# The product of probabilities and values in two attentions: high and low parts of the transposed probabilities side by side in one matmul, the halves summed by a VectorE reduction

## The chip, the core and the metric

The kernel runs on one NeuronCore of a Trainium2 chip. The metric is the device time of one execution in microseconds (us), taken as the median over several executions; lower is better. The kernel before takes 2276.8 us (three runs, 2276.53 to 2277.06). The core has engines that run in parallel and wait for each other through semaphores: TensorE (PE in the profile; PEld is its weight load), VectorE (DVE), ScalarE (ACT), GpSimd (POOL), and SyncE (SP), which issues most of the DMAs. Each engine works through its own instructions in the order in which the program lists them.

## What is computed

Two layers of an encoder on 1024 tokens of width 1024, in float32. Layer 0 mixes tokens with multi-head latent attention (mixer A), layer 1 with differential attention (mixer B); both have 8 heads, values of width 128, and a mask by chunks of 64 tokens. After each mixer and each SwiGLU there is a residual and a LayerNorm. Cut to the attentions:

```
# mixer A
logits = einsum(q_nope, k_nope) + einsum(q_rope, k_rope)
p = softmax(where(chunk_mask, logits * scale, -1e30))
o = einsum('bhqk,bkhd->bqhd', p, v)          # then o @ w_o
...
# mixer B
p = softmax(where(chunk_mask, logits * scale - slope * dist, -1e30))   # two maps per head
a = p[:, 0] - lam * p[:, 1]
o = einsum('bhqk,bkhe->bqhe', a, v)          # then rmsnorm(o) @ w_o
...
h = layernorm(ALPHA * h + mix)
h = layernorm(ALPHA * h + swiglu(h))
```

The change concerns the two products of the probabilities with the values v.

## The kernel before

**High and low parts.** TensorE's operands here have the type fp32r (so named in the profile's rows). Each operand x is split into a high part (x copied to fp32r by ScalarE) and a low part (x minus the high part, by VectorE or GpSimd), and a product becomes three matmuls that add into one PSUM tile: high by high, high by low, low by high.

**Stages.** The program runs through the latent projections, attention A (from 94 us to about 350 us of the profile), its output projection and layer 0's SwiGLU, attention B (from 1145 to about 1552 us), its output projection and layer 1's SwiGLU.

**One attention.** `attention` (L268) walks over heads h and blocks i of 128 queries, 64 steps in all. For each step there are three pieces:

- `score` (L1281 for A, L1428 for B) calls `softmax_block` (L216). PE multiplies queries by keys into PSUM tiles tagged "s"; DVE adds the bias and takes the running maximum (L229), which frees the "s" tile; ACT takes the exponential (L232); DVE the reciprocal of the sum (L234); in A, POOL scales the row (L1290), in B, POOL and DVE combine the two maps (L1440, L1441).
- `turn` calls `transpose_block` (L237). PE transposes the 128x128 probability blocks into a PSUM tile (L160), ACT copies them out as the high part (L253), DVE subtracts to give the low part (L254). Before, the two parts are two SBUF tiles, `pth` and `ptl`, each [128, 2 key blocks, 256 queries].
- `mix` (L1296 and L1447) runs once for every two query blocks, that is for each group g of 256 queries. It calls `pv_group` (L256), which goes over the nj = 2g+2 key blocks that the mask lets through; each has three matmuls with 256 columns into one PSUM tile [128, 256]: vh by hi, vh by lo, vl by hi. The last key block concerns only the second half of the queries, so its three matmuls have 128 columns. Over 8 heads and g = 0 to 3 there are 160 key blocks in each attention, 32 of them last ones.

The PSUM tile is then read out. In A, ACT copies it (L1300) to an SBUF tile `ob` (two buffers), which a DMA on SP's queue stores to `o_dr`. In B, DVE copies it (L1450) to the resident `bo`, from which ACT squares it for the norm (L1465). The product's PSUM tiles come from `ps_o` (L123): in A from the three buffers tagged "m", which the projections use too, in B from a single buffer tagged "o". All of these PSUM tiles are 512 columns wide, of which the product used 256.

**What sets the order.** The program is written with a tile framework. It places each instruction on its engine by a simulated timeline and by priorities (`high_priority` at L280 and L282), so that the pieces of several steps, and the projections of the next head that `fill` hands in, are woven together; when durations or dependencies of some pieces differ, the places of others move too. On each engine the resulting order is fixed, and an instruction that waits holds up all that stand behind it on that engine.

Of the kernel before, what the change touches and what calls it, by code (L numbers as in the profile page):

```python
# [10 lines left out]
F32R = mybir.dt.float32r  # L11
AF = mybir.ActivationFunctionType
ALU = mybir.AluOpType
# [3 lines left out]
P = 128  # L17
# [25 lines left out]
def trunk(  # L43
# [33 lines left out]
    V, A, G, T = nc.vector, nc.scalar, nc.gpsimd, nc.tensor  # L77
# [45 lines left out]
    def ps_o(name):  # L123
        return ps.tile([P, 512], F32, tag="o", bufs=ps_bufs[3], name=name) if len(ps_bufs) > 3 else ps_m(name)
# [112 lines left out]
    def transpose_block(ptp, pts, l, i, name):  # L237
        qc = (i % 2) * P
        for jq in range(i // 4 + 1):
            nj = min(4, i + 1 - 4 * jq)  # L240
            pt = ps_t(f"pt_{name}_{jq}")
            for jj in range(nj):
                j = 4 * jq + jj
                tr(pt[:, jj * P:(jj + 1) * P], l[:, j * P:(j + 1) * P])
            for jp in range(2 * jq, 2 * jq + (nj + 1) // 2):
                n = min(2, i + 1 - 2 * jp)
                if i % 2 == 0:
                    pts[jp] = tuple(
                        ptp.tile([P, 2, 256], F32R, tag=f"pt{c}", name=f"pt{c}_{name}_{jp}") for c in "hl"
                    )  # L250
                src = pt[:, (jp % 2) * 256:(jp % 2) * 256 + n * P].rearrange("p (j q) -> p j q", j=n)
                hv, lv = (t[:, :n, qc:qc + P] for t in pts[jp])
                newest["hi"] = A.copy(hv, src).ins  # L253
                newest["lo"] = V.tensor_tensor(lv, src, f32(hv), ALU.subtract).ins  # L254

    def pv_group(pts, g, v_of, name):  # L256
        po = ps_o(f"o_{name}")
        nj = 2 * g + 2
        for j in range(nj):
            hi, lo = pts[j // 2]  # L260
            vh, vl = v_of(j)
            c = slice(P, 256) if j == nj - 1 else slice(0, 256)
            first, last = j == 0, j == nj - 1
            for a, b, st, sp_ in ((vh, hi, first, False), (vh, lo, False, False), (vl, hi, False, last)):
                T.matmul(po[:, c], a, b[:, j % 2, c], start=st, stop=sp_, skip_group_check=True)
        return po

    def attention(score, turn, mix, fill, la, hp):  # L268
# [918 lines left out]
    lv = [late[:, 64 * i:64 * i + 64] for i in range(4)]  # L1187
# [16 lines left out]
    with ast as st:  # L1204
# [3 lines left out]
        ptp = st.enter_context(tc.tile_pool(name="a1p", bufs=5, side="right", reuse_waits="tile"))  # L1208
        vt, qr, qn, kn, wts, lt, pts = {}, {}, {}, {}, {}, {}, {}
# [86 lines left out]
        def mix_a(h, g):  # L1296
            hc = slice((h % 2) * P, (h % 2) * P + P)
            po = pv_group(pts.pop((h, g)), g, lambda j: tuple(v[:, hc] for v in vt[h // 2, j]), f"a{h}_{g}")
            ob = vp.tile([P, 256], F32, tag="ob", name=f"ob{h}_{g}", bufs=2)
            A.copy(ob, po[:, :256])  # L1300
            nc.sync.dma_start(o_dr[0][g][h], ob)

        fill = {}
# [12 lines left out]
        for h in range(1, H):  # L1316
            b = 8 * (h - 1)
# [45 lines left out]
    with ExitStack() as st:  # L1363
        lp = st.enter_context(tc.tile_pool(name="b1l", bufs=5, reuse_waits="tile"))
        pool = st.enter_context(tc.tile_pool(name="b1", bufs=2, reuse_waits="tile"))
        ptp = st.enter_context(tc.tile_pool(name="b1p", bufs=4, reuse_waits="tile"))
        bb = pool.tile([P, S], F32, tag="bb", name="bb", bufs=1)
        nc.sync.dma_start(bb, c_bias_b)
        vt, lt, pts, sqs, q_slot = {}, {}, {}, {}, {}
        qt = [big_tile(f"bq{j}") for j in range(2)]  # L1370
        kt = [big_tile(f"bk{j}") for j in range(2)]
        ob = big_tile("bo", F32)
# [74 lines left out]
        def mix_b(h, g):  # L1447
            hc = slice((h % 2) * P, (h % 2) * P + P)
            po = pv_group(pts.pop((h, g)), g, lambda j: tuple(v[:, hc] for v in vt[h // 2, j]), f"b{h}_{g}")
            V.tensor_copy(o_rows(h, g), po[:, :256])  # L1450

        def o_rows(h, g, n=1):

            return ob[:, h % 2, g * 256:(g + n) * 256]
# [182 lines left out]
```

## Time and profile before

| | |
|---|---|
| median of 3 runs | 2276.8 us |
| the profiled execution | 2275.05 us |
| its span, first to last instruction | 2273.3 us |
| PE busy, share of the span | 2245.0 us, 99% |
| DVE busy | 1550.6 us, 68% |
| ACT busy | 1016.7 us, 45% |
| POOL busy | 862.6 us, 38% |
| mean granted TensorE clock | 0.998 of full speed |

The profile is one execution. Its times count from the start of the span. In a row of the timeline the first number is the start of an instruction and the second its duration; matmuls overlap in these rows, each starting before the one ahead of it has ended, so that what a matmul costs a busy PE is the distance from its start to the next start, and not the duration in its row. A group row ends with busy time in us, the mean duration in ns, and the idle time of the engine just before its instructions with what ended it.

### The profile page before, as it was taken

The numbers are of one execution on the slowest core, as the hardware profiler recorded it, in microseconds if no ns is written. First come the engines' busy times: TensorE is split into PE (matmuls) and PEld (weight loads), VectorE is DVE, ScalarE is ACT, GpSimd is POOL, SyncE is SP. The second block draws the span as 40 slices with busy tenths as digits, with TensorE's granted clock in tenths as the row PEclk, the third lists the DMA queues.
The fourth block names the chain that finished last, engine by engine and source line by source line (L and its number), as shares of the span: only waits on it lengthen the run. The fifth ranks groups of instructions, "written<-read, shape, count | busy, mean of one in ns | idle before, by whom it ended". The sixth has DMA issues, their size and how long they took to land. (4 is left out here: it accounts for less than half of the span.)

```text
span 2273.3 us, 31157 instructions
## 1 busy us (share of the span) xinstructions
PE 2245.0 (99%) x11426; PEld 1914.2 (84%) x11426; DVE 1550.6 (68%) x2909; ACT 1016.7 (45%) x2101; POOL 862.6 (38%) x673
## 2 busy tenths in 40 slices
PE   9999999999999999999999999999999999999998
PEld 9898998888888888888888898987778888888886
DVE  6666665596656668778476667576587666668778
ACT  4465664352333334445465656555442333334443
POOL 2233452114444446555232424221014444446562
PEclk9999999999999999999999999999999999999999
DMA  5121325334313238554310212153344223247554
GB/s 206 41 97 59 119 98 186 139 140 140 126 70 139 70 126 323 196 179 167 107 47 23 67 38 70 26 208 116 125 153 152 94 98 111 96 156 271 181 179 149
DMA packets 104281, 289.33 MB, mean 127 GB/s; under 512 B 8640, under 2 KB 31808, under 8 KB 93632
## 3 DMA queue, kind: packets, MB, share of 16 engines
q1 hardware_dynamic: 100128, 277.90, 34.8%
q0 software_dynamic: 4000, 9.44, 1.5%
q8 instruction: 90, 1.47, 0.3%
q14 instruction: 63, 0.52, 0.1%
HBM read 205.78 MB, written 77.33 MB: 125 GB/s over the span
## 5 line engine op out<-in xcount | busy, mean ns | idle before, releaser
L511 ACT CAST op_g<-gr 128x512 fp32r<-128x512 f32 x240 | 147.5, 622 | 404.7 <-PE gb L555 225.2
L511 POOL TENSOR_TENSOR op_g<-gr,op_g 128x512 fp32r<-128x512 f32 x104 | 146.0, 1408 | 300.6 <-DVE tmp L649 160.5
L511 DVE TENSOR_TENSOR op_h<-rh,op_h 128x512 fp32r<-128x512 f32 x154 | 163.7, 1092 | 61.2 <-ACT op_h L511 61.1
L555 PE MATMUL ga<-xh_m,op_g 128*128 128x512 f32 x512 | 168.1, 389 | 0.0
L511 ACT CAST op_h<-rh 128x512 fp32r<-128x512 f32 x154 | 92.5, 619 | 145.8 <-DMA rh<-h_dr 39.4
L858 PE MATMUL dw<-op_w_t,op_h 128*128 128x512 f32 x660 | 151.9, 390 | 0.0
L858 PEld LDWEIGHTS dw<-op_w_t,op_h 128*128 128x128 f32 x660 | 123.3, 188 | 25.6
L232 ACT ACTIVATE l_b<-l_b,mx_b 128x256 f32<-128x256 f32 (+7 forms) x128 | 99.5, 778 | 75.9 <-DVE mx_b L229 74.0
L511 POOL TENSOR_TENSOR op_w_t<-tt,op_w_t 128x512 fp32r<-128x512 f32 x66 | 99.9, 1516 | 82.6 <-ACT op_w_t L511 78.1
L1440 POOL TENSOR_SCALAR l_b<-l_b,r_b,cst 128x128 f32<-128x128 f32 (+3 forms) x64 | 52.5, 821 | 204.8 <-DVE r_b L234 198.8
L858 PE MATMUL dx<-op_w_b,op_h 128*128 128x512 f32 x528 | 120.3, 389 | 0.0
L858 PEld LDWEIGHTS dx<-op_w_b,op_h 128*128 128x128 f32 x528 | 99.1, 188 | 20.6
L555 PE MATMUL gc<-t1h_f,op_g 128*128 128x512 f32 x352 | 116.2, 391 | 0.0
L555 PE MATMUL gb<-t4h_f,op_g 128*128 128x512 f32 x352 | 115.7, 390 | 0.5 <-DVE tmp L640 0.5
L511 DVE TENSOR_TENSOR op_g<-gr,op_g 128x512 fp32r<-128x512 f32 x136 | 110.2, 810 | 8.7 <-ACT op_g L511 8.2
L555 PE MATMUL gc<-b22h_f,op_g 128*128 128x512 f32 x352 | 115.5, 389 | 0.0
L555 PE MATMUL gb<-t3h_f,op_g 128*128 128x512 f32 x352 | 115.2, 389 | 0.0
L555 PE MATMUL gb<-t2h_f,op_g 128*128 128x512 f32 x352 | 115.1, 389 | 0.0
L511 POOL TENSOR_TENSOR op_g<-s,op_g 128x512 fp32r<-128x512 f32 x40 | 54.7, 1368 | 156.1 <-ACT op_g L511 156.0
L555 PEld LDWEIGHTS ga<-xh_m,op_g 128*128 128x128 f32 x512 | 96.1, 188 | 19.9
L155 PE MATMUL bp<-xT_f,h_wb 128*128 128x512 f32 x256 | 102.8, 402 | 0.0
L157 PE MATMUL bp<-xT_f,l_wb 128*128 128x512 f32 x256 | 101.6, 397 | 0.0
(389 smaller groups left out, 6738.4 us busy)
## 6 DMA issues: line engine op xcount, KB each, us to landing
gr<-in_w_gu SPq DMA_DIRECT2D x44, 1024.0 KB, 6.8
rh<-h_dr SPq DMA_DIRECT2D x28, 1024.0 KB, 5.2
h_dr<-sh SPq DMA_DIRECT2D x22, 1024.0 KB, 4.9
h_dr<-hp SPq DMA_DIRECT2D x22, 768.0 KB, 4.0
tt<-in_w_dn SPq DMA_DIRECT2D x22, 512.0 KB, 8.3
rh<-h_dr SPq DMA_DIRECT2D x14, 768.0 KB, 4.3
z<-xs_dr SPq DMA_DIRECT2D x16, 512.0 KB, 11.2
rw_b<-in_w_dn SPq DMA_DIRECT2D x8, 1024.0 KB, 8.8
```

Of the source, the lines that this page charges most:

```text
L155: T.matmul(ps_out, lh, rh, start=(i == 0), stop=False)
L157: T.matmul(ps_out, ll, rh, start=False, stop=(i == n - 1))
L232: newest["exp"] = A.activation(l[:, :n], l[:, :n], AF.Exp, bias=mx, scale=-1.0, accum_out=sm).ins
L511: return A.copy(hi, src).ins, eng.tensor_tensor(lo, src, f32(hi), ALU.subtract).ins
L555: T.matmul(o, w[:, a, kc], x[b][:, k, :], start=(first and k == 0 and (a, b) == (0, 0)), stop=(k == 3 and a == 1), skip_group_check=True,)
L858: i = T.matmul(o, h[:, a, c], w[:, b_], start=(first and (a, b_) == (0, 0)), stop=(last and a == 1), skip_group_check=True,).ins
L1440: G.tensor_scalar(l1[:, :n], l1[:, :n], r1, nlam, ALU.mult, ALU.mult)
```

## The change

The high and low parts become one SBUF tile `pt` of shape [128, 2 parts, 2 key blocks, 256 queries]. For each key block, one matmul with vh as weights takes both parts as its moving operand (two runs of 256 columns) and writes 512 columns of PSUM: the first 256 hold vh by hi, the second 256 vh by lo. A second matmul with vl as weights adds vl by hi to the first 256 columns. For the last key block the two matmuls have 2x128 and 128 columns. So there are 640 matmuls where there were 960, with as many columns as before. The halves are summed when the tile is read out, by one VectorE `tensor_reduce` over 512 columns whose innermost step is from one half to the other; it replaces ACT's copy in A and DVE's copy in B.

```
--- before.py
+++ after.py
@@ -245,24 +245,21 @@
             for jp in range(2 * jq, 2 * jq + (nj + 1) // 2):
                 n = min(2, i + 1 - 2 * jp)
                 if i % 2 == 0:
-                    pts[jp] = tuple(
-                        ptp.tile([P, 2, 256], F32R, tag=f"pt{c}", name=f"pt{c}_{name}_{jp}") for c in "hl"
-                    )
+                    pts[jp] = ptp.tile([P, 2, 2, 256], F32R, tag="pt", name=f"pt_{name}_{jp}")
                 src = pt[:, (jp % 2) * 256:(jp % 2) * 256 + n * P].rearrange("p (j q) -> p j q", j=n)
-                hv, lv = (t[:, :n, qc:qc + P] for t in pts[jp])
+                hv, lv = (pts[jp][:, a, :n, qc:qc + P] for a in range(2))
                 newest["hi"] = A.copy(hv, src).ins
                 newest["lo"] = V.tensor_tensor(lv, src, f32(hv), ALU.subtract).ins
 
     def pv_group(pts, g, v_of, name):
-        po = ps_o(f"o_{name}")
+        po = ps_o(f"o_{name}").rearrange("p (a q) -> p a q", a=2)
         nj = 2 * g + 2
         for j in range(nj):
-            hi, lo = pts[j // 2]
+            pt = pts[j // 2][:, :, j % 2]
             vh, vl = v_of(j)
             c = slice(P, 256) if j == nj - 1 else slice(0, 256)
-            first, last = j == 0, j == nj - 1
-            for a, b, st, sp_ in ((vh, hi, first, False), (vh, lo, False, False), (vl, hi, False, last)):
-                T.matmul(po[:, c], a, b[:, j % 2, c], start=st, stop=sp_, skip_group_check=True)
+            T.matmul(po[:, :, c], vh, pt[:, :, c], start=(j == 0), stop=False, skip_group_check=True)
+            T.matmul(po[:, 0, c], vl, pt[:, 0, c], start=False, stop=(j == nj - 1), skip_group_check=True)
         return po
 
     def attention(score, turn, mix, fill, la, hp):
@@ -1297,7 +1294,7 @@
             hc = slice((h % 2) * P, (h % 2) * P + P)
             po = pv_group(pts.pop((h, g)), g, lambda j: tuple(v[:, hc] for v in vt[h // 2, j]), f"a{h}_{g}")
             ob = vp.tile([P, 256], F32, tag="ob", name=f"ob{h}_{g}", bufs=2)
-            A.copy(ob, po[:, :256])
+            V.tensor_reduce(ob, po.rearrange("p a q -> p q a"), mybir.AxisListType.X, ALU.add)
             nc.sync.dma_start(o_dr[0][g][h], ob)
 
         fill = {}
@@ -1447,7 +1444,7 @@
         def mix_b(h, g):
             hc = slice((h % 2) * P, (h % 2) * P + P)
             po = pv_group(pts.pop((h, g)), g, lambda j: tuple(v[:, hc] for v in vt[h // 2, j]), f"b{h}_{g}")
-            V.tensor_copy(o_rows(h, g), po[:, :256])
+            V.tensor_reduce(o_rows(h, g), po.rearrange("p a q -> p q a"), mybir.AxisListType.X, ALU.add)
 
         def o_rows(h, g, n=1):
```

Each product on PE goes from three instructions to two. This is PE in attention A, head 0, group 1: `o_a_1` is the group's PSUM tile, `pth`, `ptl` and `pt` are the transposed probabilities, `vh` and `vl` the values of one key block. Before:

```order
L265 MATMUL o_a_1_1261<-pth_a_2_0_1167,vh_0_1030 128x256
L265 MATMUL o_a_1_1261<-ptl_a_2_0_1168,vh_0_1030 128x256
L265 MATMUL o_a_1_1261<-pth_a_2_0_1167,vl_0_1031 128x256
L265 MATMUL o_a_1_1261<-pth_a_2_0_1167,vh_1_1041 128x256
L265 MATMUL o_a_1_1261<-ptl_a_2_0_1168,vh_1_1041 128x256
L265 MATMUL o_a_1_1261<-pth_a_2_0_1167,vl_1_1042 128x256
L265 MATMUL o_a_1_1261<-pth_a_2_1_1171,vh_2_1182 128x256
L265 MATMUL o_a_1_1261<-ptl_a_2_1_1172,vh_2_1182 128x256
L265 MATMUL o_a_1_1261<-pth_a_2_1_1171,vl_2_1183 128x256
L265 MATMUL o_a_1_1261<-pth_a_2_1_1171,vh_3_1193 128x128
L265 MATMUL o_a_1_1261<-ptl_a_2_1_1172,vh_3_1193 128x128
L265 MATMUL o_a_1_1261<-pth_a_2_1_1171,vl_3_1194 128x128
```

And now:

```order
L261 MATMUL o_a_1_1256<-pt_a_2_0_1164,vh_0_1029 128x512
L262 MATMUL o_a_1_1256<-pt_a_2_0_1164,vl_0_1030 128x256
L261 MATMUL o_a_1_1256<-pt_a_2_0_1164,vh_1_1040 128x512
L262 MATMUL o_a_1_1256<-pt_a_2_0_1164,vl_1_1041 128x256
L261 MATMUL o_a_1_1256<-pt_a_2_1_1167,vh_2_1177 128x512
L262 MATMUL o_a_1_1256<-pt_a_2_1_1167,vl_2_1178 128x256
L261 MATMUL o_a_1_1256<-pt_a_2_1_1167,vh_3_1188 128x2x128
L262 MATMUL o_a_1_1256<-pt_a_2_1_1167,vl_3_1189 128x128
```

Four key blocks had twelve matmuls and have eight; the last block's three of 128 columns are one of 2x128 and one of 128.

The start of a product moves as well. This is PE in attention A, head 3, group 3, where the projection `qn` of the next head is woven in. Before, the first matmul, which needs the high part alone, stood ahead of nine projection matmuls, and the matmul on the low part behind them:

```order
L160 MATMUL pt_a_7_1_2420<-ident,l_a_7_2278 128x128 x4
L265 MATMUL o_a_3_2438<-pth_a_6_0_2363,vh_0_1715 128x256
L155 MATMUL qn_0_2511<-c_111,h_wa_4_2507 128x512
L156 MATMUL qn_0_2511<-c_113,h_wa_4_2507 128x512
L157 MATMUL qn_0_2511<-c_111,l_wa_4_2508 128x512
L155 MATMUL qn_0_2511<-c_111,h_wa_4_2507 128x512
L156 MATMUL qn_0_2511<-c_113,h_wa_4_2507 128x512
L157 MATMUL qn_0_2511<-c_111,l_wa_4_2508 128x512
L155 MATMUL qn_0_2511<-c_111,h_wa_4_2507 128x512
L156 MATMUL qn_0_2511<-c_113,h_wa_4_2507 128x512
L157 MATMUL qn_0_2511<-c_111,l_wa_4_2508 128x512
L265 MATMUL o_a_3_2438<-ptl_a_6_0_2364,vh_0_1715 128x256
```

Now the first matmul needs both parts, and the group starts with four matmuls ahead of the projection:

```order
L226 MATMUL s_a_3_0_2396<-ck_lo,qr_1_0_1621 128x512
L261 MATMUL o_a_3_2356<-pt_a_6_0_2285,vh_0_1680 128x512
L262 MATMUL o_a_3_2356<-pt_a_6_0_2285,vl_0_1681 128x256
L261 MATMUL o_a_3_2356<-pt_a_6_0_2285,vh_1_1741 128x512
L262 MATMUL o_a_3_2356<-pt_a_6_0_2285,vl_1_1742 128x256
L155 MATMUL qn_0_2420<-c_111,h_wa_4_2416 128x512
```

The transposes `pt_a_7_1`, which stood ahead of the group, come behind it here.

On DVE the readout of A is new. This is DVE in attention A between heads 4 and 5: `r_a` is the reciprocal of the sum, `ql` and `kn` low parts of projections, `l_a` with `mx_a` the readout of a score tile. Before:

```order
L234 RECIPROCAL r_a_7_3219<-sm_a_7_3217 128x1
L1260 TENSOR_TENSOR ql_1_3316<-qn_1_3305,qh_1_3315 128x512
L1274 TENSOR_TENSOR kn_5_3091<-kn_1_3351,kn_5_3090 128x512
L229 ISA l_a_0_3266,mx_a_0_0_3273<-s_a_0_0_3267,ba 128x128
L229 ISA mx_a_0_0_3273 128x1
L254 TENSOR_TENSOR ptl_a_6_0_3286<-pt_a_6_0_3280,pth_a_6_0_3285 128x2x128
```

And now:

```order
L234 RECIPROCAL r_a_7_3087<-sm_a_7_3085 128x1
L1257 TENSOR_TENSOR ql_1_3174<-qn_1_3163,qh_1_3173 128x512
L1271 TENSOR_TENSOR kn_5_2966<-kn_1_3209,kn_5_2965 128x512
L1297 TENSOR_REDUCE ob_2_3125<-o_a_2_3112 128x256
L229 ISA l_a_0_3128,mx_a_0_0_3135<-s_a_0_0_3129,ba 128x128
L229 ISA mx_a_0_0_3135 128x1
L252 TENSOR_TENSOR pt_a_6_0_3147<-pt_a_6_0_3142,pt_a_6_0_3147 128x2x128
```

The reduction of group 2 stands in front of the score readout of the next head, and everything behind it on DVE waits until PE has finished that group's matmuls. ACT no longer has the copy L1300.

More of the change, by code (lines that the diff above doesn't have):

```diff
@@ L256, in pv_group @@
     def pv_group(pts, g, v_of, name):
-        po = ps_o(f"o_{name}")
+        po = ps_o(f"o_{name}").rearrange("p (a q) -> p a q", a=2)
         nj = 2 * g + 2
         for j in range(nj):
-            hi, lo = pts[j // 2]
+            pt = pts[j // 2][:, :, j % 2]
             vh, vl = v_of(j)
             c = slice(P, 256) if j == nj - 1 else slice(0, 256)
-            first, last = j == 0, j == nj - 1
-            for a, b, st, sp_ in ((vh, hi, first, False), (vh, lo, False, False), (vl, hi, False, last)):
-                T.matmul(po[:, c], a, b[:, j % 2, c], start=st, stop=sp_, skip_group_check=True)
+            T.matmul(po[:, :, c], vh, pt[:, :, c], start=(j == 0), stop=False, skip_group_check=True)
+            T.matmul(po[:, 0, c], vl, pt[:, 0, c], start=False, stop=(j == nj - 1), skip_group_check=True)
         return po
@@ L1299, in mix_a @@
             ob = vp.tile([P, 256], F32, tag="ob", name=f"ob{h}_{g}", bufs=2)
-            A.copy(ob, po[:, :256])
+            V.tensor_reduce(ob, po.rearrange("p a q -> p q a"), mybir.AxisListType.X, ALU.add)
             nc.sync.dma_start(o_dr[0][g][h], ob)
```

8 lines of the change are left out of this document (3 added, 5 removed).

## The prediction

> **What bounds the kernel now.** First the page's head, for the shares; then the table of busy time by stretch, over attention A (94 to 350 us), a piece of layer 0's SwiGLU, and attention B (1145 to 1552 us).
>
> ```profile
> span 2273.3 us, 31157 instructions
> ...
> PE 2245.0 (99%) x11426; PEld 1914.2 (84%) x11426; DVE 1550.6 (68%) x2909; ACT 1016.7 (45%) x2101; POOL 862.6 (38%) x673
> ```
>
> ```profile
> core 0: us, PE busy (x) PEld busy (x) DVE busy (x) ACT busy (x) POOL busy (x), PEclk, DMA share, GB/s
> 94.00:350.00 256.00, 253.25 (x1661) 231.00 (x1661) 176.53 (x510) 164.29 (x409) 108.39 (x95) 1.00 0.29 98
> 520.00:620.00 100.00, 100.00 (x443) 82.83 (x442) 65.77 (x78) 29.71 (x50) 45.64 (x32) 1.00 0.37 128
> 1145.00:1552.00 407.00, 401.91 (x2451) 355.01 (x2450) 282.36 (x837) 237.32 (x551) 126.94 (x123) 1.00 0.21 68
> ```
>
> PE is idle for 256.00 - 253.25 = 2.8 us of attention A and 407.00 - 401.91 = 5.1 us of attention B. Both stages last as long as PE has matmuls, so a matmul that becomes cheaper there shortens the kernel, unless PE then waits. The engine to watch is DVE, at 69% in both (176.5 of 256, 282.4 of 407). Next, what PE waits for at the very matmuls of the change, from the view of line 265:
>
> ```profile
> its engine sat idle before it (us, times) until:
>   DVE ptl_b L254: 2.8, 5
>   ACT pth_a L253: 2.3, 4
>   ACT pth_b L253: 1.0, 3
>   DVE ptl_a L254: 0.9, 2
> who waited for it (us, times):
>   DVE bo L1450: 11.8, 9
>   ACT ob L1300: 5.5, 8
> ```
>
> In all, 7.0 us in 14 waits: the operands nearly always lie ready. On the other side it is the readouts that wait for PE, not PE for them.
>
> **The change, part by part.** The sum is made against the profiled execution, 2275.05 us. What the matmuls cost now is read from the starts in the timeline: thirteen 256-column matmuls of one product from 293.34 us (the first and the last are shown, and what follows), and the end of the same product with its three 128-column ones.
>
> ```profile
> 293.34 0.28 PE L265 MATMUL o_a<-pth_a,vh 128*128 128x256 f32 x1
> ...
> 294.78 0.28 PE L265 MATMUL o_a<-pth_a,vh 128*128 128x256 f32 x1
> 294.90 0.34 PE L226 MATMUL s_a<-ck_lo,qr 128*128 128x384 f32 x1
> ...
> 298.73 0.28 PE L265 MATMUL o_a<-pth_a,vl 128*128 128x256 f32 x1
> 298.85 0.22 PE L265 MATMUL o_a<-pth_a,vh 128*128 128x128 f32 x1
> 298.91 0.28 PE L265 MATMUL o_a<-ptl_a,vh 128*128 128x128 f32 x1
> 299.02 0.27 PE L265 MATMUL o_a<-pth_a,vl 128*128 128x128 f32 x1
> 299.13 0.51 PE L226 MATMUL s_a<-kn,qh 128*128 128x320 f32 x2
> ```
>
> A 256-column matmul costs (294.90 - 293.34) / 13 = 0.120 us. A 512-column one costs 100.00 / 443 = 0.2257 us, from the SwiGLU row above, where PE ran 512-column matmuls without a gap. Twice 0.120 is more than 0.2257: two separate matmuls cost 14 ns more than one with the columns of both. The three 128-column ones cost 299.13 - 298.85 = 0.28 us, a mean of 0.093, far over half of 0.120.
>
> *Full key blocks.* There are 2 x (160 - 32) = 256. Each cost 3 x 0.120 = 0.360 us and will cost 0.2257 + 0.120 = 0.346: 256 x 0.0143 = **3.7 us less**. The new matmul reads two runs of 256 columns that lie apart, which no row of this trace does on PE. At best that is free; at worst it costs what its two parts cost now, 0.240, and saves nothing. I take the 512-column row, since it has the same number of columns and one weight load.
>
> *Last key blocks.* There are 64. The three take 0.28 us; the new pair takes 0.120 for 2x128 columns, and for the single 128-column one between 0.06 (298.85 to 298.91) and 0.11 (298.91 to 299.02). I take the mean of the three, 0.093: 64 x (0.28 - 0.213) = **4.3 us less**, with ends of 64 x 0.05 = 3.2 and 64 x 0.10 = 6.4.
>
> Here a rule speaks against the change. The Trainium skill, in "TensorE: Matmul & The Clock Gate", section "Back-to-back issue gap", gives the isolated warm gap as columns / 2.4 + 2.5 ns. By it the three matmuls of a full block take 327.5 ns and the new two 325.0, and the whole change would save under 1 us. The rows above disagree, with 93 ns for 128 columns where the formula has 56 and 120 for 256 where it has 109; the same section says that in a stream with weight loads the formula falls short at small sizes, and this trace bears that out.
>
> *The readout.* DVE reduces 512 columns of PSUM. The nearest rows are the other DVE instruction that reads 512 columns of PSUM, the copy of 256, and the one reduction in the program, of 64 columns. The rows of line 254 and of ACT's copy are for what follows.
>
> ```profile
> L229 DVE CUSTOM_DVE_ANT_0 l_b<-s_b,bb 128x512 f32<-128x512 f32 x32 | 21.7, 678 | 0.1
> L254 DVE TENSOR_TENSOR ptl_a<-pt_a,pth_a 128x256 fp32r<-128x256 f32 x128 | 52.1, 420 | 14.8 <-ACT pth_a L253 13.5
> L254 DVE TENSOR_TENSOR ptl_b<-pt_b,pth_b 128x256 fp32r<-128x256 f32 x128 | 51.9, 419 | 13.4 <-ACT pth_b L253 12.6
> L1450 DVE COPY bo<-o_b 128x256 f32<-128x256 f32 x32 | 13.4, 419 | 12.1 <-PE o_b L265 11.8
> L1300 ACT COPY ob<-o_a 128x256 f32<-128x256 f32 x32 | 12.0, 376 | 10.7 <-PE o_a L265 5.5 <-issue 3.7 <-ACT pth_a L253 0.7
> ```
>
> ```profile
> L1199 DVE TENSOR_REDUCE edge<-edge x2: 220/220/220, 31.9 to 33.4; 128x1 f32<-128x64 f32 x2
> ```
>
> From 256 to 512 columns DVE needs (678 - 419) / 256 = 1.01 ns a column, over a fixed 160; the reduction of 64 columns, 220, lies on the same line (160 + 65). So 0.68 us. The innermost step, from one half to the other, is one that no row shows: if each column took two turns it would be 160 + 512 x 2.02 = 1.19 us; the other end is 0.42, no dearer than the copy. I take 0.68. DVE gets 32 x 0.68 = 21.8 us more in A (69% becomes 77%) and 32 x (0.68 - 0.42) = 8.3 us more in B (71%): 30.1 us. ACT loses 12.0 us, for which nobody waited.
>
> How much of the 30.1 reaches PE? Behind the reduction on DVE stand the score readouts (L229) and the low parts (L254 before, L252 now), and PE waits for both. Line 254 kept PE waiting 2.8 + 0.9 = 3.7 us at the products for 104 us of work, 3.6%. Its waits at the score tiles of A are as small:
>
> ```profile
> PEld s_a L226 <- DVE mx_a L229: 1.8, 3, 1.1
> ...
> PE s_a L226 <- DVE mx_a L229: 1.1, 2, 0.9
> ```
>
> A fuller queue makes more of each late microsecond, so I take 5%: **1.5 us more**. The ends are nothing and all of it.
>
> *The first matmul of a product now needs the low part.* The seven waits on ACT above (3.3 us) become waits for DVE's part, later by 0.42 less the 0.12 of the matmul that ran meanwhile: 7 x 0.30 = 2.1 us if nothing else moved. But the listing of head 3 shows the product standing at another place relative to the work around it, which can as well cover the 3.7 us of waits for the low part. I take 0, ends -3.7 and +2.1.
>
> *What moves with the readout.* In A the reduction also waits for `ob`, free once its store of two groups ago has landed. On ACT that wait was once long:
>
> ```profile
> L1300 ACTq EVENT_SEMAPHORE  x30: 17/17/2512, 115.6 to 354.4; - x30
> ```
>
> 2.5 us, once, would now block DVE's queue. PE has matmuls of other steps to go on with; I take 0, at most 2.5. At the end of B the last readout is on the path to the norm: 0.68 - 0.42 = **0.3 us more**. The single "o" tile in B is free 0.3 us later, and the 32 groups are 407 / 32 = 12.7 us apart: 0. Layer 1's SwiGLU keeps its instructions, but DVE's order at its start shifts by single instructions around a wait that PE has there:
>
> ```profile
> 1656.96 0.73 PE L555 MATMUL ga<-xh_m,op_gp 128*128 128x512 f32 x2 [1.94 <-DVE op_gp L511]
> ```
>
> It may go or as much come on top: 0, ends -1.9 and +1.9.
>
> *Sum*: -3.7 - 4.3 + 1.5 + 0.3 = -6.2 us, so 2275.05 becomes 2268.9. The median of the runs lies 1.75 us above the profiled execution; with the same distance, 2276.8 - 6.2 = **2270.6 us**.
>
> **The rivals.** A measurement here tells about 0.2% from no change, 4.6 us: faster means under 2272.2, slower over 2281.4.
>
> *DVE gives it back.* If 20% rather than 5% of DVE's added time reaches PE, 6.0 us return: -8.0 + 0.3 + 6.0 = -1.7, **2275.1 us**. For it: the reductions stand ahead of score readouts, as listed, and A has just two "s" tiles. Against it: the 3.6% above. From 10% on ((8.0 - 0.3 - 4.6) / 30.1) my forecast turns into no change.
>
> *The step across the halves doubles the reduction, and DVE falls behind* (the slower side). At 1.19 us DVE gets 32 x 1.19 + 32 x 0.77 = 62.7 us more; A's DVE is then at 84%. With the share of 5% that costs 3.1 us and the change still gains; it decides from a share of 20% on ((8.0 - 0.3 + 4.6) / 62.7). With 30%: -8.0 + 0.3 + 18.8 = +11.1, **2287.9 us**. For it: nothing on DVE reads with such a step now. Against it: DVE has 80 us free in A, and PE's small waits. The Trainium skill, "Advanced Engine Details and Errata", section "PSUM Cachelines", says that every two consecutive elements should be contiguous for best throughput, which these are not; no run here shows it yet.
>
> *PE gains nothing.* Either the two-run matmul costs what its parts did, or PE's time goes by columns alone, and the columns are as many as before. Then 0 + 1.5 + 0.3 = +1.8, **2278.6 us**. Against the second stand the rows of 0.120 and 0.093; the first is open. The second is close to what the formula of the Trainium skill cited above would give.
>
> **How the numbers follow.** Forecast 0.57 (its own range, from the ends of the matmul terms and a share under 10%, 2266.5 to 2272.2), DVE gives it back 0.22, PE gains nothing 0.07, doubled reduction 0.14. So faster 0.57, same 0.22 + 0.07 = 0.29, slower 0.14. The low end is the best matmul terms (-3.7 - 6.4) with little given back and part of SwiGLU's wait gone: 2266. The high end takes in both cases of no change with their bounds (the low-part and `ob` waits): 2281; it leaves out the slower case and a sliver below.
>
> **What would show it.** Right: in the profile after, 512-column matmuls of the product 0.226 us ahead of the next start, the last pair near 0.21; the reduction at 0.68 us; PE busy down by 8 us over both attentions, and idle up by no more than 2. Wrong: 0.24 between starts (PE gains nothing); a reduction of 1.2 us; PE waiting on L229 or L252 for several us in A (DVE gives it back); or a stage without the change, such as layer 1's SwiGLU, moving by more than 2 us.

## The result, and the profile after

The change makes the kernel slower. The changed kernel takes 2284.3 us (median of 6 runs, 2283.3 to 2285.5) where the kernel before takes 2276.8 (6 runs, 2276.3 to 2277.6): a ratio of 1.0032, with a 95% interval of 1.0022 to 1.0041, some 7.5 us. The forecast was 2270.6, and its range ended at 2281. The profiled execution took 2284.48 us, against 2275.05 before, so the two traces can stand for the runs.

First the head of the page of the changed kernel, and its table of busy time over the two attentions, with the stretches and columns of the table before.

```profile
span 2282.7 us, 30498 instructions
...
PE 2241.2 (98%) x11106; PEld 1895.1 (83%) x11106; DVE 1571.3 (69%) x2941; ACT 1004.2 (44%) x2069; POOL 861.8 (38%) x673
```

```profile
94.00:350.00 256.00, 249.25 (x1501) 221.10 (x1499) 190.02 (x541) 152.15 (x376) 108.34 (x95) 1.00 0.31 101
...
1145.00:1552.00 407.00, 398.96 (x2283) 345.31 (x2281) 287.37 (x825) 233.21 (x545) 127.67 (x121) 1.00 0.22 67
```

PE has less work (2241.2 us busy, 2245.0 before) in a span that is 9.4 us longer: it is idle more. (Busy time fell by 3.8 us only, although the product matmuls got cheaper by 10.6, as shown below; other matmuls cost more now, a part of them at half clock, see the last section.) The waits at the merged matmul itself don't explain it. From the view of its line:

```profile
its engine sat idle before it (us, times) until:
  DVE pt_b L252: 4.2, 5
  DVE pt_a L252: 2.7, 5
```

That is 6.9 us, as many as the 7.0 before, all of it on the low part now. (The view counts the waits of PE and of its weight loads apart, so that one stop can stand in it twice; PE alone has 2.6 us now and had 2.1.) Nor do the two sizes that the forecast guessed explain it. The reductions, from the groups by shape, and one product's end in attention B, from PE's timeline:

```profile
L1447 DVE TENSOR_REDUCE bo<-o_b 128x256 f32<-128x512 f32 x32 | 22.0, 687 | 5.2 <-PE o_b L262 4.7
L1297 DVE TENSOR_REDUCE ob<-o_a 128x256 f32<-128x512 f32 x32 | 21.8, 687 | 6.1 <-PE o_a L262 5.9
```

```profile
1332.79 0.40 PE L261 MATMUL o_b<-pt_b,bvh 128*128 128x512 f32 x1
1333.02 0.28 PE L262 MATMUL o_b<-pt_b,bvl 128*128 128x256 f32 x1
1333.14 0.28 PE L261 MATMUL o_b<-pt_b,bvh 128*128 128x256 f32 x1
1333.26 0.23 PE L262 MATMUL o_b<-pt_b,bvl 128*128 128x128 f32 x1
1333.32 0.27 PE L226 MATMUL s_b<-bk,bq 128*128 128x128 f32 x1
```

The reduction takes 0.687 us where 0.68 was forecast. From start to start, the merged matmul of 512 columns takes 0.23 us, its partner 0.12, and the last block's pair 0.12 + 0.06 = 0.18. Added up over all product matmuls (each from its start to the next start on PE, less the idle time in between), the products took 58.5 us in A and 58.2 in B before, and 53.0 and 53.1 now: 10.6 us saved, more than the 8.0 of the forecast.

So where did 9.4 + 10.6 = 20 us go? The starts of the stages on PE show it: the first score of an attention, its last product matmul, and the first matmul of what follows. Before:

```profile
81.37 0.33 PE L226 MATMUL s_a<-kn,qh 128*128 128x128 f32 x1 [0.38 <-ACT kn L1273]
...
348.49 0.28 PE L265 MATMUL o_a<-pth_a,vl 128*128 128x128 f32 x1
348.61 0.44 PE L155 MATMUL zp_a<-wo,oh_a 128*128 128x512 f32 x1
...
1128.25 0.33 PE L226 MATMUL s_b<-bk,bq 128*128 128x128 f32 x2
...
1550.39 0.28 PE L265 MATMUL o_b<-pth_b,bvl 128*128 128x128 f32 x1
...
1626.27 0.39 PE L430 MATMUL zp_a<-who,oh_a 128*128 128x512 f32 x1
...
1627.30 0.48 PE L555 MATMUL ga<-xh_m,op_gp 128*128 128x512 f32 x1
```

And after:

```profile
81.76 0.49 PE L226 MATMUL s_a<-kn,qh 128*128 128x128 f32 x2 [0.38 <-ACT kn L1270]
...
346.86 0.22 PE L262 MATMUL o_a<-pt_a,vl 128*128 128x128 f32 x1
...
351.43 0.79 PE L155 MATMUL zp_a<-wo,oh_a 128*128 128x512 f32 x1 [4.34 <-ACT oh_a L310]
...
1132.56 0.33 PE L226 MATMUL s_b<-bk,bq 128*128 128x128 f32 x2
...
1559.13 0.22 PE L262 MATMUL o_b<-pt_b,bvl 128*128 128x128 f32 x1
...
1634.95 0.39 PE L427 MATMUL zp_a<-who,oh_a 128*128 128x512 f32 x1
...
1637.90 0.50 PE L552 MATMUL ga<-xh_m,op_gp 128*128 128x512 f32 x1 [1.68 <-ACT zp_a L182]
```

Attention A is 2.0 us shorter (267.12 to 265.10). Behind it PE stands still for 4.34 us before the output projection. Attention B is 4.4 us longer (422.14 to 426.57), though its matmuls are 5 us cheaper. And the start of layer 1's SwiGLU comes 2.95 us behind the projection instead of 1.02.

**The end of A.** SP's and POOL's queues there, from the timeline. Before:

```profile
342.62 0.38 SPq L309 DMA_DIRECT2D of_a<-o_dr  x1
...
343.31 0.76 POOL L164 DMA_DIRECT2D mg<-in_ln_mix_g  x1 [0.15 <-issue]
344.07 0.55 POOL L164 DMA_DIRECT2D mb<-in_ln_mix_b  x1
```

After, SP, POOL, and what ACT waits for:

```profile
340.45 0.93 SPq L317 DMA_DIRECT2D zy_a<-in_x  x2
341.81 1.38 SPq L306 DMA_DIRECT2D of_a<-o_dr  x2
```

```profile
340.91 0.76 POOL L164 DMA_DIRECT2D mg<-in_ln_mix_g  x1 [0.26 <-PE s_a L226]
341.67 0.55 POOL L164 DMA_DIRECT2D mb<-in_ln_mix_b  x1
```

```profile
350.75 1.14 ACT L310 CAST oh_a<-of_a 128x512 fp32r<-128x512 f32 x2 [5.30 <-DMA of_a<-o_dr]
```

`of_a` is what the output projection starts from. Before, it was issued ahead of the LayerNorm rows `mg` and `mb`; now four transfers of 0.5 MB (two z tiles, `mg`, `mb`) stand ahead of it, and ACT has it 8.9 us after its issue (350.75 - 341.81), where the first one landed after 4.0 before. Nothing in the change touches these lines; the scheduler moved them.

**Attention B.** By the table of busy time over B from its first score to its last product, PE is idle for 10.4 us there, where it was 5.1. One of the new waits, with DVE's rows first, then POOL's and PE's:

```profile
1333.52 0.69 DVE L1447 TENSOR_REDUCE bo<-o_b 128x256 f32<-128x512 f32 x1 [1.08 <-PE o_b L262]
1334.13 2.87 DVE L1438 SCALAR_TENSOR_TENSOR l_b<-l_b,r_b,l_b 128x1024 f32<-128x1024 f32 x1
1337.03 0.68 DVE L1423 TENSOR_TENSOR bk<-bp,bk 64x512 fp32r<-64x512 f32 x1
...
1338.16 0.27 DVE L229 CUSTOM_DVE_ANT_0 l_b<-s_b,bb 128x128 f32<-128x128 f32 x1
```

```profile
1333.51 2.41 POOL L147 TENSOR_TENSOR l_wb<-r_wb,h_wb 128x1024 fp32r<-128x1024 f32 x1
```

```profile
1338.49 0.44 PE L226 MATMUL s_b<-bk,bq 128*128 128x384 f32 x1 [1.64 <-DVE mx_b L229]
```

The reduction at the head of DVE's queue waits 1.08 us for PE's product; behind it come the combination of the two maps, 2.87 us, and only then the score readout that frees PE's next tile. The combination takes 1.29 us in the other seven places with this size; here it runs while POOL splits a weight. The kernel before had no wait of PE at this place, and none of its combinations took over 1.64 us.

### The profile page after: what moved, and what is told of

Its sections match the earlier page's. It is cut to its first block, busy times and chain, and to the rows that moved or that the text cites. A ratio compares the mean times of both kernels' runs of the same rounds, so it can differ in the third digit from the quotient of the medians.

```text
span 2282.7 us, 30498 instructions
## 1 busy us (share of the span) xinstructions
PE 2241.2 (98%) x11106; PEld 1895.1 (83%) x11106; DVE 1571.3 (69%) x2941; ACT 1004.2 (44%) x2069; POOL 861.8 (38%) x673
## 5 line engine op out<-in xcount | busy, mean ns | idle before, releaser
L155 PE MATMUL bp<-xT_f,h_wb 128*128 128x512 f32 x256 | 101.7, 397 | 0.0
L156 PE MATMUL bp<-xT_f,h_wb 128*128 128x512 f32 x256 | 101.7, 397 | 0.0
```

Of the source, the lines that this page charges most:

```text
L155: T.matmul(ps_out, lh, rh, start=(i == 0), stop=False)
L156: T.matmul(ps_out, lh, rl, start=False, stop=False)
```

## The experiments

Three theories. *Order*: the cheaper matmuls are real, and what was lost was lost because the scheduler put all engines' instructions in another order. *VectorE load*: the 30 us of reductions hold up what PE waits for. *First matmul*: a product now starts only when its low part is there.

To keep operations and order apart, most kernels below carry a table `ORDER` with the place of every instruction on its engine, taken from the kernel before ("old order") or from the changed kernel ("new order"), and a function that ties each instruction behind its neighbour. The tie is one of order alone; waits for data stay what they were. The kernel before was not run tied to its own order; the nearest to it is attention A of e8 below, which has the old operations in the old order and is 1.1 us longer than in the kernel before.

```
+    def pinned(table):
...
+            for p, q in zip(row, row[1:]):
+                behind(mine[q], mine[p])
+
+    pinned(ORDER)
     ps_stack.close()
```

The stages of all runs, from the starts of the same matmuls as above, in us (one profiled execution each; stretches that no kernel changes differ by 1 to 2 us from execution to execution, in e8 by 3 us in layer 1's SwiGLU, so that smaller differences in one row say nothing):

| kernel | operations, order | A | end of A | B | start of SwiGLU 1 | median | against before |
|---|---|---|---|---|---|---|---|
| before | old, old | 267.12 | 0.11 | 422.14 | 1.02 | 2276.8 | |
| after | new, new | 265.10 | 4.57 | 426.57 | 2.95 | 2284.3 | +7.5 |
| e1 | new, old | 273.95 | 0.06 | 420.04 | 1.02 | 2282.2 | +5.1 |
| e2 | old, new | 267.04 | 5.13 | 431.53 | 2.95 | 2288.2 | +11.0 |
| e3 | new, new, z moved | 265.12 | 3.59 | 428.16 | 2.95 | 2281.9 | +4.7 |
| e4 | reduction alone, old | 272.04 | 0.11 | 423.12 | 1.02 | 2282.0 | +4.8 |
| e5 | new, new, four loads moved | 265.17 | 0.06 | 428.15 | 2.95 | 2280.8 | +4.0 |
| e6 | new; new order to SwiGLU 0, then old | 265.09 | 0.06 | 420.04 | 1.02 | 2272.0 | -4.8 |
| e7 | merge alone, old | 272.38 | 0.06 | 419.27 | 1.02 | 2277.9 | +1.1 |
| e8 | new in B alone, old | 268.26 | 0.11 | 420.03 | 1.02 | 2276.1 | -0.7 |
| e9 | new, low values first, old | 268.82 | 0.17 | 419.41 | 1.02 | 2276.3 | -1.2 |
| e10 | as e9, no reduction, old | 266.49 | 0.17 | 418.58 | 1.02 | 2273.2 | -4.3 |
| e11 | new, low values first, own order | 265.93 | 4.34 | 425.10 | 2.95 | 2285.0 | +7.5 |
| e12 | e6, low values first in B's first blocks | 265.15 | 0.06 | 419.55 | 1.02 | 2270.8 | -5.5 |

The last column is the difference of medians to the kernel before on the same chip.

**e1 and e2: operations and order apart.** e1 is the changed kernel with `ORDER` from the kernel before, e2 the kernel before with `ORDER` from the changed one.

> The changed kernel with its instructions pinned to the order of the kernel before, on all five engines: each merged matmul stands where the high-by-low matmul of its key block stood (the first of a product where that product's first matmul stood), and the reduction of attention A stands on VectorE at the place in time that ScalarE's copy had. Nothing else is changed. Theory 'order' (the cheaper matmuls are real, and the time was lost because the scheduler wove another order round them): about 10 us of matmul time saved (256 full blocks x 0.015, 64 last blocks x 0.10) and at most 3 us given back, so 2267 to 2270 us. Rival 'VectorE load' (30 us of reductions hold up score readouts and low parts): the waits stay, 2277 to 2284. Rival 'first matmul' (each product now starts only when the low part is there): up to 64 x 0.3 = 19 us of possible waits against 10 saved, of which a third would give 2273.

Measured: 2282.2 us, ratio 1.0022 (1.0013 to 1.0031).

> The kernel before, pinned to the order of the changed kernel: three matmuls a key block stand where the two stood, ScalarE's copy of attention A stands at the place in time of the reduction, VectorE's copy of attention B in that reduction's place. 'Order': the new order costs its 17 us without the saving of 10, so 2290 to 2295 us. 'VectorE load': without the reductions the waits go, so about 2277 to 2280. 'First matmul': the low part is again not needed at once, about 2277.

Measured: 2288.2 us, ratio 1.0050 (1.0038 to 1.0063).

e2 shows that the new order by itself costs 11 us. In its profiled execution, 2.8 us above the median, it is 5.0 at the end of A, 9.4 in B, 1.9 at the start of layer 1's SwiGLU, and nothing in A. But e1 lies where 'VectorE load' put it, so 'order' as I had stated it falls: in the old order the new operations cost 5 us as well. B gains 2.1 there; A loses 6.8. What PE waits for in e1's A is seen in the view of its product tile `o_a`, from the list of what the engines waited for there (us and times, PE and its weight loads each counted; L625 is here the low part's line), and at one product in PE's timeline:

```profile
  DVE pt_a L625: 15.9, 20
```

```profile
216.04 0.50 PE L634 MATMUL o_a<-pt_a,vh 128*128 128x512 f32 x1 [0.88 <-DVE pt_a L625]
```

In the kernel before, the low part kept the products of A waiting 0.9 us in all by the same count. PE alone waits 5.7 us in 8 places in e1, where it was 0.3 in one. That is the third theory's wait, and it asked for the two kernels e7 and e4 (each part alone) and for e9.

**e4: the reduction alone**, in the old order. The three matmuls a key block stay:

```
-            for a, b, st, sp_ in ((vh, hi, first, False), (vh, lo, False, False), (vl, hi, False, last)):
-                T.matmul(po[:, c], a, b[:, j % 2, c], start=st, ...)
+            for a, b, k, st, sp_ in ((vh, hi, 0, first, False), (vh, lo, 1, first, False), (vl, hi, 0, False, last)):
+                T.matmul(po[:, k, c], a, b[:, j % 2, c], start=st, ...)
```

Both halves are started in the first key block here, one after the other, and the output is not the full sum; the instructions, their sizes and their waits are the ones to be timed.

> The kernel before, in its own order, with the readout of the changed kernel alone: the three matmuls a key block stay, but the one on the low part adds into the second half of the PSUM tile, and VectorE's reduction sums the halves (in A at the place in time of ScalarE's copy, which goes). 30 us more on VectorE, nothing saved on TensorE. 'Order': 0 to 2 us more than before, 2276.8 to 2279. 'VectorE load': 5 to 17 us more, 2282 to 2294. 'First matmul': no change, since the first matmul still needs the high part alone, 2277.

Measured: 2282.0 us, ratio 1.0019 (1.0010 to 1.0028). 'VectorE load' at its low end: 4.9 us in A, 1.0 in B. By these stages 5.9 of the 30.1 us added to DVE came through to PE, 20%, but not all of it is shown to be the reductions' doing. PE's two longest new stops in A, 2.0 us together, are at projections `v` that wait for a PSUM tile; in A the product's tile is one of the three "m" tiles that the projections use, and in e4 it is the reduction that frees it:

```profile
236.67 0.39 PE L536 MATMUL v<-h_wa,c 128*128 128x256 f32 x1 [1.00 <-DVE ob L1681]
```

Yet e7 and e10 below, which have no reduction, stop at `v` in the same two places, for 2.0 and 1.9 us. Here is the second in e10:

```profile
235.43 0.39 PE L527 MATMUL v<-h_wa,c 128*128 128x256 f32 x1 [0.97 <-DVE vl L1615]
```

What these runs share is a DVE instruction just ahead (the low part `qr`) that took 2.1 us where it took 0.69 in the kernel before, because of a meeting with POOL (last section). Without these 2.0 us some 3.9 of the 30.1 are left, an estimate: 13 to 20%. The rest shows at score readouts (PE waited 1.8 us for them, 1.1 before) and low parts.

**e7: the merge alone**, in the old order, with the readouts of the kernel before.

```
-            V.tensor_reduce(ob, po.rearrange("p a q -> p q a"), mybir.AxisListType.X, ALU.add)
+            A.copy(ob, po[:, 0])
...
-            V.tensor_reduce(o_rows(h, g), po.rearrange("p a q -> p q a"), mybir.AxisListType.X, ALU.add)
+            V.tensor_copy(o_rows(h, g), po[:, 0])
```

> The merged matmuls in the order of the kernel before (placed as in e1), with the readouts of the kernel before: ScalarE's copy in A, VectorE's copy in B, of the first half alone. The product of high values and low probabilities is thus computed and left out of the output. 'VectorE load': without the reductions only the 10.6 us of cheaper matmuls are left, 2266 to 2269. 'First matmul': in e1 TensorE waited some 5.8 us in A for the low part (pt_a L252 of the changed kernel) at products; if those waits are not the reductions' doing they stay, and the time is 2271 to 2274.

Measured: 2277.9 us, ratio 1.0008 (0.9999 to 1.0017): worse than either theory said. With no reduction at all, A is still 5.3 us longer than before (2.0 of them the two stops at `v`), and the wait for the low part stays. The same row of the view of `o_a`:

```profile
  DVE pt_a L624: 14.5, 20
```

So those waits are not the reductions' doing (PE alone: 5.0 us in 8 places). B gains 2.9.

**e9, e10 and e11: low values first.** If the first matmul of a product is the trouble, the one that needs the high part alone can go first:

```
-            T.matmul(po[:, :, c], vh, pt[:, :, c], start=(j == 0), stop=False, ...)
-            T.matmul(po[:, 0, c], vl, pt[:, 0, c], start=False, stop=(j == nj - 1), ...)
+            T.matmul(po[:, 0, c], vl, pt[:, 0, c], start=(j == 0), stop=False, ...)
+            T.matmul(po[:, :, c], vh, pt[:, :, c], start=False, stop=(j == nj - 1), ...)
```

> As e1 (merged matmuls, reductions, the order of the kernel before), but of each key block's two matmuls the one on the low values, which needs the high probabilities alone, comes first: it stands where high by high stood, and the merged one where high by low stood. 'First matmul': the waits of A for the low part at the start of a product go, and what is left is the reductions' 5.9 us (e4: 4.9 in A, 1.0 in B) against 10.6 of cheaper matmuls: 2271 to 2274 us. 'VectorE load': the low parts are late because VectorE is, TensorE waits at the second matmul as it did at the first, 2279 to 2283 as e1.

Measured: 2276.3 us, ratio 0.9996 (0.9987 to 1.0005).

> As e9, with the readouts of the kernel before (a copy of the first half alone, so that the product of high values and low probabilities is left out of the output, as in e7). 'First matmul': 10.6 us of cheaper matmuls and nothing against them, 2266 to 2269. 'VectorE load' has no reductions to point to here; if e7's loss had another cause than the first matmul, 2275 to 2279 as e7.

Measured: 2273.2 us, ratio 0.9981 (0.9972 to 0.9990).

Both moved as 'first matmul' says, and both stopped short of its numbers. Against e1, A is 5.1 us shorter in e9; against e7 it is 5.9 shorter in e10, and the waits for the two parts, in the view of `o_a` in e10 (L623 is ACT's high part, L624 the low one), are near those of the kernel before:

```profile
  ACT pt_a L623: 3.2, 5
  DVE pt_a L624: 1.1, 3
```

What is missing is in part a price that the exchange brings along. With the merged matmul at the end, the last block's pair costs more, here in e10:

```profile
300.51 0.23 PE L633 MATMUL o_a<-pt_a,vl 128*128 128x128 f32 x1
300.57 0.33 PE L634 MATMUL o_a<-pt_a,vh 128*128 128x256 f32 x1
300.74 0.46 PE L598 MATMUL s_a<-kn,qh 128*128 128x320 f32 x2
```

That is 0.06 + 0.17 = 0.23 us instead of 0.18, and 64 of them make 3.2 us. Added up as above, the products of e10 cost 56.0 us in A and 55.8 in B, so that only 4.9 of the 10.6 us are left of the saving. The two stops at `v` are in e9 and e10 as well, 2.2 and 1.9 us.

> The changed kernel with the two matmuls of each key block exchanged as in e9, woven by the scheduler without any table. 'First matmul': the scheduler may start a product as early as in the kernel before, and the time comes under that of the changed kernel by several us, 2272 to 2279. 'Order': the weave is new again, and what it costs is not tied to the first matmul: anywhere from 2272 to 2290, decided by the end of A and by B.

Measured: 2285.0 us, ratio 1.0039 (1.0026 to 1.0051). With its own freedom the scheduler makes nothing of the earlier start: the end of A (4.3 us) and B (+3.0) lose again. 'First matmul' missed here: in the scheduler's own order the first matmul was not what decided.

**e3 and e5: the end of A.** e3 puts z back behind `of_a`; e5 also moves `mg` and `mb`, in the table alone, behind the two weight splits that follow them on POOL.

```
+                od = nc.sync.dma_start(of, ...)
...
+                zd = nc.sync.dma_start(z, ...)
+                if prev is None or prev[0] == LAST_ORDER[0]:
+                    behind(zd.ins, od.ins)
```

> The changed kernel with one thing of the order restored: on SyncE the loads of z for the first two token blocks of layer 0's output projection stand behind the loads of of_a again, as in the kernel before. 'Order': the idle 4.3 us of TensorE at the end of attention A and most of the half-speed 6.8 us behind it go, so 4.5 to 7 us less than the changed kernel: 2277.5 to 2280. 'VectorE load' and 'first matmul': the idle time at the end of A comes from late work in attention, of_a is no earlier, 2283 to 2285.

Measured: 2281.9 us, ratio 1.0022 (1.0013 to 1.0032). A miss: PE's idle time there fell from 4.3 to 3.4 us only. `mg` and `mb` were still issued at 341.1 and 341.9, ahead of `of_a` at 342.0.

> The changed kernel pinned to its own order, with four DMA issues moved at the end of attention A: on SyncE the loads of z stand behind the loads of of_a (as in e3), and on GpSimd the two LayerNorm rows mg and mb (0.5 MB each) stand behind the two weight splits that follow them, so that they leave after of_a and not about 1 us ahead of it. 'Order': it was these 2 MB in the DMA queues, not z alone, that made of_a land late, so the idle time of 4.3 us and the half-speed stretch behind it go: 4 to 6 us less than the changed kernel, 2278.5 to 2280.5. Rival: of_a is late because the stores of o_dr ahead of it, behind the slower readout, are late; then it stays as e3 left it, 2282 to 2284.

Measured: 2280.8 us, ratio 1.0016 (1.0008 to 1.0025), 3.5 us less than the changed kernel by the medians. The wait is gone. SP's row of e5, then PE's:

```profile
341.52 0.37 SPq L679 DMA_DIRECT2D of_a<-o_dr  x1
```

```profile
346.55 0.22 PE L635 MATMUL o_a<-pt_a,vl 128*128 128x128 f32 x1
346.61 0.45 PE L528 MATMUL zp_a<-wo,oh_a 128*128 128x512 f32 x1
```

Counted from the first score of A, `of_a` is issued no earlier than in the changed kernel (260.1 us behind it in both), and is there in time: it was the company in the queues.

**e8, e6 and e12: versions that beat the kernel before.** e8 has the change in B alone, in the old order; e6 takes for each part of the changed kernel the better order; e12 is e6 with, in B, the exchange of e9 in each product's first key block only.

> Only attention B has the merged matmuls and the reduction; attention A is as in the kernel before, and every engine is pinned to the order of the kernel before. 'Order': B gains what it gained in e1, 2.2 us, and nothing else moves: 2274 to 2276. 'VectorE load': the 8 us more on VectorE in B hold TensorE up by as much as the matmuls save, 2277 or more.

Measured: 2276.1 us, ratio 1.0000 (0.9992 to 1.0009). B gained its 2.1 us in the profiled execution; in the time of the whole kernel that can't be told from nothing.

> The changed kernel, pinned up to the middle of layer 0's SwiGLU to its own order with the four moves of e5, and from there on to the order of the kernel before. If each stage keeps the time it had by itself: A 2.1 us less than the kernel before, its end as before, B 2.2 less (as in e1), nothing at the start of layer 1's SwiGLU: 2272 to 2274 us, faster than both kernels. If the order of a stage doesn't decide it ('VectorE load'), 2280 or more.

Measured: 2272.0 us, ratio 0.9981 (0.9972 to 0.9990): the sum of the stages came out.

```
+            two = [(slice(0, 2), vh), (0, vl)]
+            if name[0] == "b" and j == 0:
+                two.reverse()
```

> As e6, and in attention B the two matmuls of each product's first key block are exchanged (low values first, where high by high stood); all other blocks keep the merged matmul first, since e10 showed that the last block's pair costs 0.05 us more the other way round. 'First matmul': in B of e9 the score matmuls and transposes around the products lost 1.7 us of hidden waits against e1, and the products cost 1.9 more by the exchange of the other blocks, which isn't made here: some 2 us less than e6, 2269 to 2271. Rival: B's waits lie elsewhere (the low part is late for the second matmul as well), 2272 as e6.

Measured: 2270.8 us, ratio 0.9974 (0.9965 to 0.9984), the fastest of all; the change's operations are all in it. The 2 us that it was to gain on e6 are not shown: B is 0.5 us shorter, and the intervals overlap.

## Why the prediction was wrong

**The sign was wrong by two steps, and either was enough: the order was left out of the sum, and what the new operations make PE wait was put at 1.5 us.** With the order held, the new operations make the kernel 5.1 us slower (e1); with the old operations, the new order makes it 11.0 slower (e2). With the better of the two orders in each stage, and the four loads moved, the same operations come to 2272.0 us (e6): the saving was real, and neither order as it stood let it through.

**The order.** The part "What moves with the readout" let the order change in one place, layer 1's SwiGLU, at -1.9 to +1.9, though the listings ahead of it showed other places moving in A. There the new order took the upper end, +1.9. The other two places had no term: +4.5 at the end of A, and in B the difference between the two orders with the same operations, 426.57 - 420.04 = 6.5 (e1 against after; e2 finds it with the old operations too, 9.4). In A the new order is worth 273.95 - 265.10 = 8.9 us to the new operations, and nothing to the old ones (e2): by the view of `o_a`, the waits for the low part are 2.7 us in it and 15.9 in the old order. The prediction had announced the sign to look for, "a stage without the change moving by more than 2 us".

**Full and last key blocks**: right, and undersized. 10.6 us against 8.0. The last pair was 0.18 us, the good end given: 64 x 0.10 = 6.4 us. (The good ends together, -3.7 - 6.4, give 2266.7 and not the 2266.5 at the low end of the forecast's own range.) The row of 512 columns held within 10 ns (0.23 us where 0.2257 was taken), so the two runs side by side cost little or nothing. The formula of the Trainium skill ("TensorE: Matmul & The Clock Gate", "Back-to-back issue gap"), by which under 1 us would be saved, doesn't agree with this trace. It gives 0.3275 us for the three matmuls of a full block and 0.325 for the two, where the rows have 0.36 and 0.35; and for the last block 0.167 and 0.165, where they have 0.28 and 0.18. Most of the saving is in that last pair, and the formula has next to nothing there.

**The reduction at 0.68 us**: right, 0.687. The rival's 1.19 fell. The rule that two consecutive elements should be contiguous (the Trainium skill, "Advanced Engine Details and Errata", "PSUM Cachelines") did not price this read: with a step of 256 columns between the two elements, the reduction stays on the line of the readouts, 160 + 512 x 1.01 ns.

**"5% of it reaches PE"**: wrong, too small. e4 has 5.9 of 30.1 us, 20%, with the order held, or some 13% without the stops that runs without a reduction have as well. The 5% came from the waits at the products and the score tiles as they were; the forecast did not look at the PSUM tile that ACT had freed in 0.376 us and DVE now frees in 0.69, behind its queue, but how much this tile costs is not shown apart from the meeting with POOL. 20% is the share of the rival "DVE gives it back"; its time was wrong, since the two other terms came on top, and that the 5.9 us are so near its 6.0 is in part luck.

**"The first matmul: 0, ends -3.7 and +2.1"**: wrong. The 7 waits of the trace before were taken as the whole of it (two of PE and five of its weight loads, which can be the same stops). With the order held, A loses 5.3 us in e7 by the merge without the reductions, although its products are cheaper and only 2.0 of it are the stops at `v`, and gains 5.1 when the first matmul again needs the high part alone (e9 against e1). Those 7 were waits at an order that had been woven for a start on the high part alone; how soon behind the start the low part would be there, at all the other products, they don't tell.

**The `ob` wait**: 0 as taken. In the view of the tile `ob` after, the reductions wait for PE alone, 5.9 us. **The end of B**, put at 0.3 us more, does not show: from the last product to the last projection matmul listed above it is 75.88 us before and 75.82 after.

What stays open is why the scheduler's own order for B is 6.5 us worse than one that it had found before; one wait was followed above, the others not, and no run here shows what its simulated timeline held for true. Whether another small edit would have drawn a better order by itself wasn't tried.

## What to carry to other kernels

Where a scheduler weaves the program, an edit's price has two parts that must be measured apart: pin the old order under the new operations, and the new order under the old ones, and compare stage by stage. Look at every transfer whose issue moved, on all queues and in stages that the diff doesn't touch: here 4.5 us came from two loads on GpSimd and two on SyncE that went ahead of the one that was waited for. And when two matmuls are merged, the merged one waits for the later of its operands. Letting the one that needs the early operand alone start the group was worth 5.1 us of A in the old order, and nothing in the scheduler's own. A readout that moves to a busier engine is to be priced by what waits behind it in that engine's queue, and by the buffer that it frees.

## What the runs showed of the hardware that was not expected

*The granted clock after short pauses.* During the 4.34 us at the end of A the clock fell to half, and in B once more. The table by stretch of the changed kernel, each fall with the 3.4 to 3.6 us ahead of it (the third number from the end is the granted clock):

```profile
345.60:349.00 3.40, 1.48 (x10) 1.15 (x8) 1.06 (x3) 0.00 (x0) 2.06 (x1) 1.00 0.99 328
349.00:355.80 6.80, 4.38 (x10) 3.43 (x11) 3.19 (x5) 3.41 (x6) 0.64 (x1) 0.50 1.03 348
...
1226.00:1229.60 3.60, 1.73 (x10) 1.00 (x8) 3.06 (x11) 2.69 (x9) 1.20 (x1) 1.00 0.01 2
1229.60:1233.00 3.40, 3.04 (x12) 2.97 (x13) 2.64 (x13) 2.03 (x8) 0.45 (x1) 0.50 0.00 0
```

The Trainium skill ("TensorE: Matmul & The Clock Gate", "What's actually happening") has half speed after an idle window of about 3.4 us. If that means no matmul at all, neither fall fits. At the end of A the clock fell at 349.0, 1.9 us after the last matmul had ended, and PE had been busy for 1.48 of the 3.40 us ahead. In B, between 1223 and 1230 us, PE paused four times, and never longer than 0.96 us; it was busy for 1.73 of 3.60 us, and half speed followed for 3.4. Elsewhere the clock stayed full: the changed kernel around its pause at 1637 us, with 1.72 us busy of 3.40 (1635.9 to 1639.3), and the kernel before with one pause of 1.10 us in B, with 2.28 of 3.40 (1222.6 to 1226.0). So by these traces a stretch of some 3.4 us in which PE is a little over half idle can be enough; where the limit lies exactly they don't show. The cost, as an estimate, is half of what PE did at half clock: 2.2 us behind the end of A, which lie in the stretch between the attentions that the table of stages leaves out, and 1.5 in B.

*DVE and POOL at the same time.* The low part `qr` of 64x512 takes 0.69 us on DVE and a weight split of 128x640 1.57 us on POOL, but where the two met, one of them was held up. In the kernel before DVE started at 231.72 and POOL at 231.77: DVE took 0.69, POOL 2.07. In e4 POOL started at 233.90 and DVE at 233.91: POOL took 1.57, DVE 2.10. A few hundredths of a microsecond in the order of their starts thus decided whether POOL lost 0.5 us or DVE 1.4; in e4, what stood behind on DVE's queue then stopped PE for 1.0 us.

*The price of a matmul depends on its neighbour.* The 2x128-column matmul took 0.12 us ahead of its single 128-column partner and 0.17 ahead of the next step's work, and the single one 0.06 in both places; the same two instructions took 0.18 us in one order and 0.23 in the other.
